# A diagonal state-space scan: B and C tables laid out as [group, channel], the scan's inputs copied to PSUM four steps at a time

## The chip, the cores and the metric

The kernel runs on one core of a Trainium2 chip. The metric is the device time of one execution in microseconds (us). Times inside an execution come from one profiled execution and count from its start. The engines are TensorE (PE, and PEld for its weight loads), VectorE (DVE), ScalarE (ACT), GpSimd (POOL) and SyncE (SP), which issues most DMAs.

## The reference

An encoder of two layers over 1040 tokens of width 1024. Layer 0 mixes tokens by a bidirectional diagonal complex state-space model (S5), layer 1 by attention, and each is followed by a SwiGLU feed-forward part. The change lies in layer 0's mixer: 64 groups of 16 channels, 64 complex states in each group, a scan forward and one backward over the tokens.

```python
def s5_direction(u, lam_re, lam_im, log_dt, b_re, b_im, c_re, c_im, reverse):
    # abr, abi: the decay exp(lambda dt); bbr, bbi: B, discretised
    bu_r = jnp.einsum('blgc,gpc->blgp', u, bbr)
    bu_i = jnp.einsum('blgc,gpc->blgp', u, bbi)
    ...
    _, _, sr, si = lax.associative_scan(_s5_combine, (a_r, a_i, bu_r, bu_i), reverse=reverse, axis=1)
    return (jnp.einsum('blgp,gcp->blgc', sr, c_re) - jnp.einsum('blgp,gcp->blgc', si, c_im))

def s5_mixer(h, ...):
    y = (s5_direction(u, ..., False) + s5_direction(u, ..., True))
    y = y.reshape(bsz, L, D_MODEL) + d_skip * hf
    g = jax.nn.gelu(y, approximate=False)
    return (g * jax.nn.sigmoid(g @ w_glu)) @ w_out
```

## The kernel before

The mixer works in blocks of T = 8 tokens, of which there are NK = 130. The 128 partitions hold 64 states of the forward direction and 64 of the backward one. It has these parts, in the order in which they are written; each engine runs its own instructions strictly in that order, and semaphores make it wait for the others.

**Parameters.** `param_T` turns B and C with TensorE into tables `bT` and `cT`, laid out as [partition, channel, real or imaginary, group]; ScalarE copies them out of PSUM (line 206). GpSimd adds real and imaginary parts into `Hs` (B) and `Cs` (C). GpSimd also makes three tables for C's side (lines 106 to 111 and 303, 304), which ScalarE completes (line 307).

**G batches.** Sixteen times, for four groups each, `g_batch` makes B times powers of the decay: three multiplies on VectorE (lines 335 to 337), which read the tables of B with group and channel exchanged, and two sums (338, 339). TensorE turns the products, ScalarE copies them to `W` (345), and `x_batch` multiplies them with the tokens `U`; ScalarE copies the result to `XS` (357), the inputs of the scan, one column pair for each block of tokens. In between, `xg_copy` and `x_main` (183, 191) turn the rest of x.

**E batches.** Sixteen times, `e_batch` makes C times powers of the decay on GpSimd: lines 386, 387 and 389 are multiplies that read the tables of C with group and channel exchanged, 388 and 390 are sums. The first four stand in GpSimd's queue near the end of the G batches. The other twelve are written into the scan's loop, one in every 7.9 steps.

**The scan.** 128 steps on VectorE, each of six instructions for two halves of the groups: a multiply of the last state with the decay `SB`, which lies in PSUM, into `TA` in SBUF (line 494); `TA` plus the step's input, back into `TA` (496); the sum with the crossed part into `XS` (498), in the place of the input.

**Work inside the scan's loop.** In rounds of four groups, one in every 6.2 steps, `inside` makes the part of the output that stays within a block. Counted from its first step, a round makes `dI` on GpSimd (424); after 2 steps TensorE multiplies B's tables with E (433); after 6 steps ScalarE copies the product to `f0` and `Z` (439 to 441), and GpSimd adds `dI` (442, 443); after 8, SyncE issues eight DMAs from `Z` to `M0` (449); after 18, TensorE multiplies `M0` with `U` (455); after 21, ScalarE copies the result back to `U` (460). There is one `f0`, so a round's copy waits until GpSimd has read that of the round before; there are two `Z`, so it waits for the DMAs of the round before the last. In the second half of the scan `swap` (467, 470, 471) reverses the backward direction's states in place, four blocks at a time, with a copy over PSUM.

**After the scan**, TensorE multiplies all states with E (521), VectorE adds to `U`, and the rest of the network follows.

PSUM has eight banks: seven in the pool `s5_ps` (`bank()`), one for `SB`.

Of the kernel before, what the change touches and what calls it, by code (L numbers as in the profile page):

```python
# [9 lines left out]
FP32 = mybir.dt.float32  # L10
# [3 lines left out]
ALU = mybir.AluOpType  # L14
PSUM = bass.MemoryType.PSUM
# [4 lines left out]
G = 64  # L20
# [5 lines left out]
CH = 16  # L26
T = 8
NK = L // T


def bc(ap, dim, n):

    a = ap.unsqueeze(dim)
    shape = list(a.shape)
    shape[dim] = n
    return a.to_broadcast(shape)
# [77 lines left out]
def s5_phase(nc, tc, P, a, ident, acc, xres, ydram, late):  # L114

    V, A, PE, PO = nc.vector, nc.scalar, nc.tensor, nc.gpsimd
    ps = P("s5_ps", bufs=7, space=PSUM)

    psc = P("s5_psc", space=PSUM)

# [8 lines left out]
    tab = P("s5_tab")  # L129
    tab2 = P("s5_tab2")  # L130
# [43 lines left out]
    for k in range(2):  # L174
        nc.sync.dma_start(out=XT[64 * k:64 * k + 64],
                          in_=a["x"][0, 1008 + T * k:1008 + T * k + T, :].rearrange("t (g c) -> g t c", c=CH))
# [20 lines left out]

    def param_T(x, raw):

        PT = tab.tile([128, CH, 2, G], FP32, name=x + "T")  # L200
        for h in range(4):
            b = bank()
            for c4 in range(4):
                c = 4 * h + c4
                transpose(b[:, c4 * 128:c4 * 128 + 128], raw[:, c::CH] if x == "b" else raw[:, c * 128:c * 128 + 128])
            A.copy(out=PT[:, 4 * h:4 * h + 4], in_=b.rearrange("p (c i g) -> p c i g", c=4, g=G))
        return PT[:, :, 0], PT[:, :, 1]

    load_x(2)
    raw_c = load_param("c")  # L210
# [37 lines left out]
        x_main(p, XG0[:, 4 * p:4 * p + 4])  # L248
    Br, Bi = param_T("b", raw_b)
    x_tail()  # L250
    Hs = tab2.tile([128, CH, G], FP32, name="Hs")
    PO.tensor_tensor(out=Hs, in0=Br, in1=Bi, op=ALU.add)
    AC = pc.tile([64, 4, 128], FP32, name="AC")
    cm, nr, sh, sn, t1, t2, rden = (t[n] for n in ("cm", "nr", "sh", "sn", "t1", "t2", "rden"))
# [17 lines left out]
    b = bank()  # L272
# [40 lines left out]
    b = bank()  # L313
    transpose(b[:CH, :G], dsr)
    A.copy(out=dsk, in_=b[:CH, :G])
    Cs = tab.tile([128, CH, G], FP32, name="Cs")

    SB = psc.tile([128, 512], FP32, name="SB")[:, :256].rearrange("p (j c g) -> p j c g", j=2, g=G)
    A.copy(out=SB[:, 0], in_=bc(PW[:, 0, 8], 1, 2))
# [9 lines left out]
    def g_batch(gb):  # L329
        gs = slice(NB * gb, NB * gb + NB)  # L330
        shp = [128, NB, T, CH]
        q_r, q_s, q_d = (bc(q[:, :, gs].rearrange("p s g -> p g s"), 3, CH) for q in G3)
        h_r, h_i, h_s = (bc(h[:, :, gs].rearrange("p c g -> p g c"), 2, T) for h in (Br, Bi, Hs))
        k1, k2, k3 = (gp.tile(shp, FP32, tag=f"k{i}", name=f"k{i}") for i in range(3))
        V.tensor_tensor(out=k1, in0=h_s, in1=q_r, op=ALU.mult)
        V.tensor_tensor(out=k2, in0=h_i, in1=q_s, op=ALU.mult)
        V.tensor_tensor(out=k3, in0=h_r, in1=q_d, op=ALU.mult)
        V.tensor_tensor(out=k2, in0=k1, in1=k2, op=ALU.subtract)
        V.tensor_tensor(out=k3, in0=k1, in1=k3, op=ALU.add)
        W = gp.tile([128, NB, 2, 128], FP32, tag="W", name="W")  # L340
        for c2, src in enumerate((k2, k3)):
            b = bank()
            for j in range(NB):
                transpose(b[:, j * 128:(j + 1) * 128], src[:, j].rearrange("p s c -> p (s c)"))
            A.copy(out=W[:, :, c2, :], in_=b.rearrange("p (g m) -> p g m", g=NB))
        return W
# [32 lines left out]
    def e_batch(gb):  # L379

        gs = slice(NB * gb, NB * gb + NB)
        g0 = NB * gb % (G // 2)
        q_r, q_s, q_d = (bc(q[:, :, gs].rearrange("p s g -> p g s"), 3, CH) for q in E3)
        c_r, c_i, c_s = (bc(c[:, :, gs].rearrange("p c g -> p g c"), 2, T) for c in (Cr, Ci, Cs))
        er, ei = (Eh[2 * gb // NG][:, i, g0:g0 + NB] for i in range(2))
        PO.tensor_tensor(out=ek, in0=c_s, in1=q_r, op=ALU.mult)
        PO.tensor_tensor(out=er, in0=c_i, in1=q_s, op=ALU.mult)
        PO.tensor_tensor(out=er, in0=ek, in1=er, op=ALU.subtract)
        PO.tensor_tensor(out=ei, in0=c_r, in1=q_d, op=ALU.mult)
        PO.tensor_tensor(out=ei, in0=ei, in1=ek, op=ALU.subtract)  # L390
# [29 lines left out]
    def inside(gb):  # L420

        gs = slice(NB * gb, NB * gb + NB)
        dI = rp.tile([CH, NB, CH], FP32, tag="dI", name="dI")
        PO.tensor_tensor(out=dI, in0=bc(ident[:CH, :CH], 1, NB), in1=bc(dsk[:, gs], 2, CH), op=ALU.mult)
        yield 2

        b = bank()
        for j in range(NB):
            g = NB * gb + j
            for c2, src in enumerate((Br, Bi)):  # L430
                for d in range(2):
                    r = slice(64 * d, 64 * d + 64)
                    PE.matmul(b[32 * d:32 * d + CH, j * 128:(j + 1) * 128], src[r, :, g],
                              E(c2, g)[r].rearrange("p s c -> p (s c)"), start=(c2 == 0), stop=(c2 == 1))
        yield 6
        Z = rp.tile([CH, NB, 2 * T - 1, CH], FP32, tag="Z", name="Z", bufs=2)
        bv = b[:64].rearrange("p (g s c) -> p g s c", g=NB, s=T)
        f0 = rp.tile([CH, NB, CH], FP32, tag="f0", name="f0")
        A.copy(out=f0, in_=bv[0:16, :, 0, :])
        A.copy(out=Z[:, :, 0:T, :], in_=bv[32:48])  # L440
        A.copy(out=Z[:, :, T:, :], in_=bv[0:16, :, 1:T, :])
        PO.tensor_tensor(out=dI, in0=dI, in1=f0, op=ALU.add)
        PO.tensor_tensor(out=Z[:, :, T - 1, :], in0=Z[:, :, T - 1, :], in1=dI, op=ALU.add)
        yield 8
        M0 = rp.tile([128, NB, 128], FP32, tag="M0", name="M0", bufs=2)
        Zf = Z.rearrange("p g s c -> p g (s c)")
        for t in range(T):
            o = (T - 1 - t) * CH
            nc.sync.dma_start(out=M0[CH * t:CH * t + CH], in_=Zf[:, :, o:o + 128])
        yield Y_AT  # L450
        banks = []
        for j0 in range(0, NB, 2):
            b = bank()
            for j in range(2):
                PE.matmul(b[:, j * NK:(j + 1) * NK], M0[:, j0 + j], U[:, NB * gb + j0 + j, :], start=True, stop=True)
            banks.append(b)
        yield Y_AT + 3
        for j0, b in zip(range(0, NB, 2), banks):
            g = NB * gb + j0
            A.copy(out=U[:, g:g + 2, :], in_=b[:, :2 * NK].rearrange("p (g k) -> p g k", g=2))  # L460
# [14 lines left out]
    sw = [(lo, hi) for hi, lo in zip(cuts, cuts[1:])]  # L475
    begun = []
    halves = [slice(0, G // 2), slice(G // 2, G)]
    for i in range(2, NK):
        for gb in range(NG):
            if i == 2 + int(E_PACE * (gb - EARLY)):  # L480
# [4 lines left out]
        for gb in list(work):  # L485
            if i >= work[gb][1]:
# [2 lines left out]
                    del work[gb]  # L489
                else:  # L490
                    work[gb][1] = 3 + int(L_PACE * gb) + at
        st, nx = XS[:, i - 1], XS[:, i]
        for h, gs in enumerate(halves):
            V.tensor_tensor(out=TA[:, h], in0=SB[:, :, :, gs], in1=bc(st[:, :, gs], 1, 2), op=ALU.mult)  # L494
        for h, gs in enumerate(halves):
            V.tensor_tensor(out=TA[:, h, 0], in0=TA[:, h, 0], in1=nx[:, :, gs], op=ALU.add)  # L496
        for h, gs in enumerate(halves):
            V.tensor_tensor(out=nx[:, :, gs], in0=TA[:, h, 0], in1=TA[:, h, 1, ::-1], op=ALU.add)  # L498
        if sw and len(begun) < 2 and i > NK // 2:
            begun.append((sw[0][0], swap(*sw.pop(0))))  # L500
            next(begun[-1][1])
# [1075 lines left out]
```

## Time and profile before

| | |
|---|---|
| median of 3 runs | 2938.03 us (2931.74 to 2938.48) |
| the profiled execution, its own time | 2936.13 us |
| its span | 2934.4 us |
| busy in the span: PE, DVE, ACT, POOL | 91%, 56%, 39%, 20% |
| granted TensorE clock, mean | 0.955 of full speed |

The parameters take to 28 us, the G batches to some 111 us, the scan to some 323 us. The remaining 2600 us (the readout, GLU, attention, feed-forward parts) are bound by TensorE.

In rows of groups of instructions, "x16" is a count. In a timeline a row has the start, the time from its first start to its last end, the engine, line and operation, output and input tiles and their shape, the count of merged instructions, and in brackets the idle time before it and what ended that. Several instructions in a row on one engine overlap by some 0.07 us, so the time from start to start is shorter than the duration.

### The profile page before, as it was taken

What the parts mean: (1) busy time and instruction counts of PE and PEld (TensorE: products, weight loads), DVE (VectorE), ACT (ScalarE), POOL (GpSimd) and SP (SyncE); (2) the same over time, 40 slices, a digit from 0 to 9 for tenths busy, and PEclk for the clock granted to TensorE, in tenths of its full rate; (3) what the DMA queues carried; (4) which work ended last, traced back from release to release, by engine and by line L of the source; (5) the groups of instructions that cost most, each with busy time, mean ns of one, the idle gap of its engine ahead of it and who ended that gap; (6) DMA issues with size and microseconds to landing.
All of it is one profiled execution on the core that took longest, in us unless ns stands there. A gap on an engine that the chain in (4) does not pass through costs nothing.

```text
span 2934.4 us, 43407 instructions
## 1 busy us (share of the span) xinstructions
PE 2656.4 (91%) x17277; PEld 2551.9 (87%) x17277; DVE 1651.7 (56%) x3270; ACT 1153.1 (39%) x2138; POOL 584.0 (20%) x544
## 2 busy tenths in 40 slices
PE   5543689999999999998998998999999999999997
PEld 4432689999999999997997887888999999999996
DVE  8999545573333333337867888887364333333334
ACT  5523353432222112125557777776332121211215
POOL 3983023230000000004204343432230000000002
PEclk8865799999999999998999999999999999999998
DMA  5110375221111111111301121111111111111101
GB/s 120 27 37 16 90 228 177 72 90 63 50 49 46 44 44 44 44 44 58 102 15 37 23 48 27 45 23 60 50 42 52 51 44 51 44 51 44 44 30 58
DMA packets 124837, 167.42 MB, mean 57 GB/s; under 512 B 13499, under 2 KB 104971, under 8 KB 124635
## 3 DMA queue, kind: packets, MB, share of 16 engines
q1 hardware_dynamic: 118203, 141.22, 17.0%
q0 software_dynamic: 5712, 21.30, 2.1%
q8 instruction: 136, 2.23, 0.3%
q10 hardware_dynamic: 720, 2.13, 0.2%
q14 instruction: 66, 0.54, 0.1%
HBM read 126.41 MB, written 21.23 MB: 50 GB/s over the span
## 4 chain that ended last, share of the span: by engine, by line
PE 74%; DVE 16%; ACT 3%; issue 3%; DMA 2%; POOL 1%; SPq 0%; ACTq 0%; DVEq 0%; POOLq 0%
PE bk L682 21%; PE bk L683 21%; PE bk L684 21%; PE pv L1094 4%; PE pt L1072 3%; DVE XS L498 3%; DVE TA L496 3%; DVE mx L1052 3%; DVE pl L1085 2%; PE b L521 2%; DVE TA L494 2%; ACT ph L1080 1%; ACT P L1056 1%; DVE acc L738 1%; PE bk L904 1%
## 5 line engine op out<-in xcount | busy, mean ns | idle before, releaser
L682 PE MATMUL bk<-Hh,unit 128*128 128x348 f32 (+1 forms) x2928 | 956.3, 327 | 9.8 <-ACT Hh L772 6.2
L683 PE MATMUL bk<-Hl,unit 128*128 128x348 f32 (+1 forms) x2928 | 945.4, 323 | 1.1 <-DVE Hl L776 1.0
L684 PE MATMUL bk<-Hh,unit 128*128 128x348 f32 (+1 forms) x2928 | 943.8, 322 | 0.0
L682 PEld LDWEIGHTS bk<-Hh,unit 128*128 128x128 f32 x2928 | 555.2, 190 | 15.1 <-ACT Hh L772 5.8
L683 PEld LDWEIGHTS bk<-Hl,unit 128*128 128x128 f32 x2928 | 554.9, 190 | 6.3 <-DVE Hl L776 2.0
L684 PEld LDWEIGHTS bk<-Hh,unit 128*128 128x128 f32 x2928 | 554.8, 189 | 0.0
L846 DVE TENSOR_TENSOR sg<-sg,bk 128x348 f32<-128x348 f32 x132 | 68.1, 516 | 631.3 <-PE bk L684 623.5
L711 POOL TENSOR_TENSOR lns<-lns,lnsq 128x348 f32<-128x348 f32 (+1 forms) x72 | 70.0, 981 | 1552.2 <-ACT lnsq L709 1551.1
L682 PE MATMUL bk<-gt,unit 128*128 128x348 f32 (+1 forms) x1056 | 340.3, 322 | 0.0
L684 PE MATMUL bk<-gt,unit 128*128 128x348 f32 (+1 forms) x1056 | 338.9, 321 | 0.0
L683 PE MATMUL bk<-gt,unit 128*128 128x348 f32 (+1 forms) x1056 | 338.2, 320 | 0.0
L869 DVE TENSOR_TENSOR acc<-acc,bk 128x348 f32<-128x348 f32 (+1 forms) x480 | 237.5, 513 | 112.7 <-PE bk L684 112.7
L848 ACT CAST gt<-sg 128x348 fp32r<-128x348 f32 x132 | 63.6, 482 | 489.1 <-DVE sg L846 489.1
L1072 PE MATMUL pt<-ident,P 128*116 128x128 f32 (+1 forms) x1188 | 181.7, 279 | 44.8 <-DVE pl L1085 40.5
L1085 DVE TENSOR_TENSOR pl<-pt,ph 116x512 fp32r<-116x512 f32 (+3 forms) x340 | 204.4, 619 | 15.1 <-ACT ph L1080 13.4
L1060 POOL TENSOR_SCALAR P<-P,l 128x1044 f32<-128x1044 f32 x132 | 149.8, 1147 | 292.5 <-PE pv L1094 167.7
L1072 PEld LDWEIGHTS pt<-ident,P 128*116 128x116 f32 (+1 forms) x1188 | 133.0, 136 | 81.1 <-issue 30.7
L683 PEld LDWEIGHTS bk<-gt,unit 128*128 128x128 f32 x1056 | 198.7, 188 | 0.5 <-issue 0.2
L682 PEld LDWEIGHTS bk<-gt,unit 128*128 128x128 f32 x1056 | 198.7, 188 | 0.5 <-issue 0.2
L684 PEld LDWEIGHTS bk<-gt,unit 128*128 128x128 f32 x1056 | 198.5, 188 | 0.0
L1080 ACT CAST ph<-pt 116x512 fp32r<-116x512 f32 (+3 forms) x340 | 168.9, 535 | 74.4 <-PE pt L1072 60.1
L597 ACT CAST unit<-raw 128x1024 fp32r<-128x1024 f32 x110 | 113.1, 1046 | 212.9 <-DMA raw<-in_ffn_w_up_dram 168.4
(285 smaller groups left out, 4123.1 us busy)
## 6 DMA issues: line engine op xcount, KB each, us to landing
raw<-in_ffn_w_gate_dram SPq DMA_DIRECT2D x44, 512.0 KB
raw<-in_ffn_w_up_dram SPq DMA_DIRECT2D x44, 512.0 KB
raw<-in_ffn_w_down_dram SPq DMA_DIRECT2D x44, 512.0 KB
y<-xdram SPq DMA_DIRECT2D x16, 520.0 KB
QA<-QH SPq DMA_DIRECT2D x30, 260.0 KB
raw<-in_attn_w_qkv_dram SPq DMA_DIRECT2D x14, 512.0 KB
xdram<-acc SPq DMA_DIRECT2D x32, 130.0 KB
xres<-xn POOLq DMA_DIRECT2D x8, 520.0 KB, 5.1
```

Source lines behind the costliest of these rows:

```text
L496: V.tensor_tensor(out=TA[:, h, 0], in0=TA[:, h, 0], in1=nx[:, :, gs], op=ALU.add)
L498: V.tensor_tensor(out=nx[:, :, gs], in0=TA[:, h, 0], in1=TA[:, h, 1, ::-1], op=ALU.add)
L597: A.copy(out=u[:, 0], in_=r)
L682: mm(out, wh, xh, start=(first and i == 0), stop=False)
L683: mm(out, wh, xl, start=False, stop=False)
L684: mm(out, wl, xh, start=False, stop=(last and i == n - 1))
L869: V.tensor_tensor(out=x, in0=x, in1=b, op=ALU.add)
L1060: PO.tensor_scalar(out=k.P, in0=k.P, scalar1=k.l, scalar2=1.0, op0=ALU.mult, op1=ALU.mult)
L1072: PE.transpose(b[:m, w * i + 128 * x:w * i + 128 * x + 128], u.P[x][:, KB_N * kt:KB_N * kt + m], self.ident)
L1080: A.copy(out=u.ph[s][:m, :w], in_=u.t[s][:m, :w])
L1085: V.tensor_tensor(out=u.pl[s][:m, :w], in0=u.t[s][:m, :w], in1=u.ph[s][:m, :w].bitcast(FP32), op=ALU.subtract)
L1094: PE.matmul(u.o[:, :u.w], VAs[u.j][:m, kt], (u.ph, u.pl)[x][s][:m, c:c + u.w], start=(kt == 0 and x == 0), stop=(kt == KBS - 1 and x == 1))
```

## The change

The tables of B and C, `Hs` and `Cs` are laid out as [group, channel], with channels next to each other; ScalarE's copy in `param_T` writes them in that order. The slices in `g_batch`, `e_batch` and the matmul of `inside` follow.

A new function `inputs` lets ScalarE copy the scan's inputs of four steps from `XS` into a PSUM tile of one bank, of which there are two. It is called for steps 2 to 5 ahead of the loop, and at every fourth step i (2, 6, 10 and so on) for steps i + 4 to i + 7, behind the other work of step i. The scan's first add puts `TA` plus the input back into that PSUM tile, and the second adds that and the crossed half of `TA` into `XS`. For the two banks, the pool `s5_ps` shrinks from seven to five.

```diff
-    ps = P("s5_ps", bufs=7, space=PSUM)
+    ps = P("s5_ps", bufs=5, space=PSUM)
...
-        PT = tab.tile([128, CH, 2, G], FP32, name=x + "T")
+        PT = tab.tile([128, 2, G, CH], FP32, name=x + "T")
...
-            A.copy(out=PT[:, 4 * h:4 * h + 4], in_=b.rearrange("p (c i g) -> p c i g", c=4, g=G))
-        return PT[:, :, 0], PT[:, :, 1]
+            A.copy(out=PT[:, :, :, 4 * h:4 * h + 4], in_=b.rearrange("p (c i g) -> p i g c", c=4, g=G))
+        return PT[:, 0], PT[:, 1]
...
-        h_r, h_i, h_s = (bc(h[:, :, gs].rearrange("p c g -> p g c"), 2, T) for h in (Br, Bi, Hs))
+        h_r, h_i, h_s = (bc(h[:, gs], 2, T) for h in (Br, Bi, Hs))
...
-        c_r, c_i, c_s = (bc(c[:, :, gs].rearrange("p c g -> p g c"), 2, T) for c in (Cr, Ci, Cs))
+        c_r, c_i, c_s = (bc(c[:, gs], 2, T) for c in (Cr, Ci, Cs))
...
+    IN = {}
+
+    def inputs(i):
+
+        n = min(4, NK - i)
+        t = psc.tile([128, 4, 2, G], FP32, tag="in", name="IN", bufs=2)
+        A.copy(out=t[:, :n], in_=XS[:, i:i + n])
+        for k in range(n):
+            IN[i + k] = t[:, k]
+
+    inputs(2)
     for i in range(2, NK):
...
-        st, nx = XS[:, i - 1], XS[:, i]
+        if i % 4 == 2 and i + 4 < NK:
+            inputs(i + 4)
+        st, nx, bi = XS[:, i - 1], XS[:, i], IN.pop(i)
         for h, gs in enumerate(halves):
             V.tensor_tensor(out=TA[:, h], in0=SB[:, :, :, gs], in1=bc(st[:, :, gs], 1, 2), op=ALU.mult)
         for h, gs in enumerate(halves):
-            V.tensor_tensor(out=TA[:, h, 0], in0=TA[:, h, 0], in1=nx[:, :, gs], op=ALU.add)
+            V.tensor_tensor(out=bi[:, :, gs], in0=TA[:, h, 0], in1=bi[:, :, gs], op=ALU.add)
         for h, gs in enumerate(halves):
-            V.tensor_tensor(out=nx[:, :, gs], in0=TA[:, h, 0], in1=TA[:, h, 1, ::-1], op=ALU.add)
+            V.tensor_tensor(out=nx[:, :, gs], in0=bi[:, :, gs], in1=TA[:, h, 1, ::-1], op=ALU.add)
```

The order of GpSimd's and TensorE's instructions stays as it was. ScalarE's queue early in the scan's loop, before the change, from the first round's Z on (line 439 copies a round's f0, 440 and 441 its Z):

```order
L440 COPY Z_1333<-b_1287 16x4x128
L441 COPY Z_1333<-b_1287 16x4x112
L439 COPY f0_1405<-b_1363 16x64
L440 COPY Z_1404<-b_1363 16x4x128
L441 COPY Z_1404<-b_1363 16x4x112
L439 COPY f0_1487<-b_1439 16x64
L440 COPY Z_1486<-b_1439 16x4x128
L441 COPY Z_1486<-b_1439 16x4x112
```

and with it, from the same place (line 484 copies inputs into PSUM, here for steps 14, 18, 22 and 26 and the three behind each):

```order
L440 COPY Z_1339<-b_1291 16x4x128
L441 COPY Z_1339<-b_1291 16x4x112
L484 COPY IN_1354<-XS_391 128x512
L484 COPY IN_1406<-XS_391 128x512
L439 COPY f0_1415<-b_1371 16x64
L440 COPY Z_1414<-b_1371 16x4x128
L441 COPY Z_1414<-b_1371 16x4x112
L484 COPY IN_1472<-XS_391 128x512
L439 COPY f0_1499<-b_1449 16x64
L440 COPY Z_1498<-b_1449 16x4x128
L441 COPY Z_1498<-b_1449 16x4x112
L484 COPY IN_1513<-XS_391 128x512
```

The input copies of the scan now stand between the rounds' copies: that for steps 22 to 25 behind the second round's f0 and Z, that for steps 26 to 29 behind the third round's.

VectorE's queue, the last sum of the G batches and the scan's first step, before:

```order
L338 TENSOR_TENSOR k1_1151<-k0_1150,k1_1151 128x512
L339 TENSOR_TENSOR k2_1152<-k0_1150,k2_1152 128x512
L494 TENSOR_TENSOR TA_1261<-SB_384,XS_391 128x128 x2
L496 TENSOR_TENSOR TA_1261<-TA_1261,XS_391 128x64 x2
L498 TENSOR_TENSOR XS_391<-TA_1261 128x2x32 x2
```

and after:

```order
L338 TENSOR_TENSOR k1_1151<-k0_1150,k1_1151 128x512
L339 TENSOR_TENSOR k2_1152<-k0_1150,k2_1152 128x512
L507 TENSOR_TENSOR TA_1261<-SB_384,XS_391 128x128 x2
L509 TENSOR_TENSOR IN_1262<-TA_1261,IN_1262 128x2x32 x2
L511 TENSOR_TENSOR XS_391<-IN_1262,TA_1261 128x2x32 x2
```

Nothing moved here; SB and IN lie in PSUM, TA and XS in SBUF, so each instruction of a step now has one input from either memory.

## Rows read from the trace of the kernel before

**Rows 1.** The chain that ended last, 0 to 345 us, its shares by line
```profile
by line: DVE XS L498 23.4%; DVE TA L496 21.7%; DVE TA L494 14.8%; issue 7.8%; PE b L521 6.2%; DVE k L337 4.4%; DVE k L336 3.5%; DVE k L335 3.4%; DMA XT<-in_x_dram 2.9%; DVE k L338 2.3%; DVE k L339 2.2%; PE b L126 0.7%; SPq L167 0.7%; SPq L1
```
**Rows 2.** Table by stretches: length, busy PE, PEld, DVE, ACT, POOL (instructions), clock, DMA
```profile
115.00:210.00 95.00, 43.33 (x430) 32.57 (x426) 94.02 (x163) 18.65 (x47) 89.58 (x93) 0.73 0.13 28
...
280.00:323.00 43.00, 14.12 (x100) 11.15 (x100) 42.87 (x269) 25.89 (x56) 3.13 (x9) 0.58 0.17 44
```
**Rows 3.** The same for line 494 alone: length, busy DVE (instructions, two a step)
```profile
115.00:210.00 95.00, 13.11 (x55) 0.73 0.13 28
...
250.00:280.00 30.00, 6.65 (x28) 0.56 0.13 27
```
**Rows 4.** The scan's three lines, the whole scan: duration min/median/max in ns
```profile
L494 DVE TENSOR_TENSOR TA<-SB,XS x256: 271/276/292, 115.4 to 322.0; 128x128 f32<-128x128 f32 x128
...
L496 DVE TENSOR_TENSOR TA<-TA,XS x256: 205/211/2996, 116.5 to 322.3; 128x64 f32<-128x64 f32 x128
...
L498 DVE TENSOR_TENSOR XS<-TA x256: 208/211/2966, 117.7 to 322.6; 128x64 f32<-128x64 f32 x128
```
**Rows 5.** Timeline, VectorE and GpSimd in one step from 128 us
```profile
128.38 1.38 POOL L389 TENSOR_TENSOR E<-cT,E 128x512 f32<-128x512 f32 x1
...
128.82 1.15 DVE L496 TENSOR_TENSOR TA<-TA,XS 128x64 f32<-128x64 f32 x2
129.84 1.26 POOL L390 TENSOR_TENSOR E<-E,ek 128x512 f32<-128x512 f32 x1
```
**Rows 6.** Timeline, VectorE in one step from 312 us, with GpSimd idle
```profile
312.42 0.47 DVE L494 TENSOR_TENSOR TA<-SB,XS 128x128 f32<-128x128 f32 x2
312.82 0.34 DVE L496 TENSOR_TENSOR TA<-TA,XS 128x64 f32<-128x64 f32 x2
313.08 0.34 DVE L498 TENSOR_TENSOR XS<-TA 128x64 f32<-128x64 f32 x2
313.36 0.47 DVE L494 TENSOR_TENSOR TA<-SB,XS 128x128 f32<-128x128 f32 x2
```
**Rows 7.** Lines of the G batches, duration min/median/max in ns
```profile
L335 DVE TENSOR_TENSOR k<-Hs,G x16: 1047/1058/2064, 28.2 to 106.2; 128x512 f32<-128x512 f32 x16
...
L337 DVE TENSOR_TENSOR k<-bT,G x16: 1056/1330/3079, 30.1 to 108.3; 128x512 f32<-128x512 f32 x16
...
L338 DVE TENSOR_TENSOR k<-k,k x16: 668/670/1712, 31.1 to 109.5; 128x512 f32<-128x512 f32 x16
```
**Rows 8.** Timeline, ScalarE in the G batches: starts of two and two rounds
```profile
79.76 0.63 ACT L191 COPY acc<-b 128x512 f32<-128x512 f32 x1
...
83.63 0.66 ACT L191 COPY acc<-b 128x512 f32<-128x512 f32 x1
...
92.91 1.13 ACT L345 COPY W<-b 128x512 f32<-128x512 f32 x2 [1.05 <-PE b L126]
...
97.44 1.13 ACT L345 COPY W<-b 128x512 f32<-128x512 f32 x2 [1.04 <-PE b L126]
```
**Rows 9.** Timeline, GpSimd: the first operations of three E batches
```profile
76.48 35.58 POOL L386 TENSOR_TENSOR ek<-Cs,E 128x512 f32<-128x512 f32 x1 [21.37 <-ACT E L307]
...
117.61 1.37 POOL L386 TENSOR_TENSOR ek<-Cs,E 128x512 f32<-128x512 f32 x1
...
124.39 1.36 POOL L386 TENSOR_TENSOR ek<-Cs,E 128x512 f32<-128x512 f32 x1
```
**Rows 10.** Timeline, ScalarE: the second round's f0, the third round's Z
```profile
151.79 0.20 ACT L439 COPY f<-b 16x64 f32<-16x64 f32 x1 [31.05 <-POOL dI L442]
...
159.00 0.58 ACT L440 COPY Z<-b 16x512 f32<-16x512 f32 x1 [5.75 <-DMA M<-Z]
```
**Rows 11.** Timeline, copies of the swaps: into PSUM, within SBUF, out of PSUM
```profile
281.11 0.59 ACT L467 COPY b<-XS 64x512 f32<-64x512 f32 x1
...
322.94 0.29 DVE L470 COPY XS<-XS 64x256 f32<-64x256 f32 x1
...
323.67 0.43 DVE L471 COPY XS<-b 64x256 f32<-64x256 f32 x1 [0.44 <-ACT XS L471]
```

More of the change, by code (lines that the diff above doesn't have):

```diff
@@ L250, in s5_phase @@
     x_tail()
-    Hs = tab2.tile([128, CH, G], FP32, name="Hs")
+    Hs = tab2.tile([128, G, CH], FP32, name="Hs")
     PO.tensor_tensor(out=Hs, in0=Br, in1=Bi, op=ALU.add)
@@ L315, in s5_phase @@
     A.copy(out=dsk, in_=b[:CH, :G])
-    Cs = tab.tile([128, CH, G], FP32, name="Cs")
+    Cs = tab.tile([128, G, CH], FP32, name="Cs")
     SB = psc.tile([128, 512], FP32, name="SB")[:, :256].rearrange("p (j c g) -> p j c g", j=2, g=G)
@@ L432, in inside @@
                     r = slice(64 * d, 64 * d + 64)
-                    PE.matmul(b[32 * d:32 * d + CH, j * 128:(j + 1) * 128], src[r, :, g],
+                    PE.matmul(b[32 * d:32 * d + CH, j * 128:(j + 1) * 128], src[r, g],
                               E(c2, g)[r].rearrange("p s c -> p (s c)"), start=(c2 == 0), stop=(c2 == 1))
```

## The prediction

> **What bounds the kernel now.** I read the chain that ended last, then a table by stretches, then single instructions. Until the readout that follows the mixer's scan the chain is almost wholly VectorE's, and the scan's three lines lead it [rows 1]. The table says why: from 115 to 210 us VectorE is never idle, yet passes only 55 / 2 = 27.5 steps, while GpSimd is busy for 89.58 of 95 us [rows 2, 3]; from 250 to 280 it passes 14. Where GpSimd has nothing to do, one step takes 313.36 - 312.42 = 0.94 us [rows 6].
>
> What VectorE does in the long steps is seen from the durations [rows 4]. The add lines 496 and 498 have a median of 211 ns and a maximum near 3 us. The multiply of line 494, with twice the elements, never takes over 292 ns in the same stretch. The difference is in the operands: line 494 reads one tensor from PSUM and one from SBUF and writes SBUF; the adds read two from SBUF. While GpSimd streams, a pair of adds is through only when the operation that GpSimd has begun is over [rows 5]. So the adds wait for GpSimd, and line 494 does not. The waits cost 95 - 27.5 x 0.94 = 69 us and 30 - 14 x 0.94 = 17 us, together 86 us of a scan whose 128 steps would take 120. GpSimd isn't slowed by this: its operations keep 1.26 to 1.38 us [rows 5, 9].
>
> **The change, part by part.** *The scan's adds.* Both adds now have one PSUM operand, so by the form of line 494 they stop waiting. Line 498's successor has exactly that form (PSUM and SBUF in, SBUF out). What an operand in PSUM costs by itself: the two multiplies of a step take 0.40 us, the two adds 0.26 [rows 6]; 2 x 64 more elements at 1.04 ns explain 0.13 of the 0.14, so reading PSUM adds nothing there. Writing PSUM from VectorE is in no row. The bound above is a copy of one shape that reads PSUM instead of SBUF, 0.43 against 0.29 us, 140 ns more [rows 11]; below, ScalarE's copies of 512 elements take 0.59 into PSUM [rows 11] and 0.58 into SBUF [rows 10], no gain to speak of. I take zero, since line 494 is the nearest row, and keep 0 to 140 ns for each of four adds.
>
> The Trainium skill speaks against this: its Perfetto Trace Analysis, section Optimizing Scalar/DVE Operations, gives a VectorE operation some 60 ns of access overhead on SBUF and some 125 on PSUM. By the difference, an estimate of 65 ns on four adds, a step would take 1.20 us and and the time would be near the middle price of the first rival below; by that rule the trace doesn't agree, since line 494's rows show no such excess.
>
> *The copies.* ScalarE gets 32 copies of 512 elements, some 0.59 us each like line 467 [rows 11], 19 us in all. It is busy 25.89 of 43 us where it has most to do [rows 2], and 11 copies more make that 32: hidden as work. But they are a new **wait**. VectorE can't begin step i + 4 before the copy that stands in ScalarE's queue behind the other work of step i, and that work waits for GpSimd. Before, ScalarE sat 31.05 us for GpSimd before the second f0 copy, and 5.75 us for the DMAs that read Z before the third Z copy [rows 10], and VectorE didn't care. Now the copy for steps 22 to 25 stands behind that f0, and the one for 26 to 29 behind that Z.
>
> This sets the scan's start, counted from the moment when GpSimd gets the port. Before, that was at 76.48 + 35.58 - 1.37 = 110.7 us [rows 9], and f0 came at 151.79, 41.1 us later, after six E batches of 6.78 us. *The tables* take the long strides from three of five operations of a batch, whose excess over the other two is 0.1 us [rows 5, 9]: 1.8 us less, 39.3. Then three copies (1.4) and the input copy (0.6): step 22 begins at 41.3. The Z copy came 159.00 - 151.79 = 7.2 us after f0; with two Z copies (1.2) and the input copy, step 26 begins at 39.3 + 7.2 + 1.8 = 48.3. The other 104 steps take 98 us: 146. GpSimd keeps just ahead: 16 batches of 6.5 us and three small operations in each of 16 rounds, 11 us, make 115 us, and its last result is asked for at step 102, at 119.7. For so small a margin I add 3 us: **149 us after GpSimd gets the port**.
>
> *The G batches.* Lines 335 to 337 read with long strides and take 1.06 to 1.33 us where line 338 takes 0.67 [rows 7]. With runs of 16 they should take 0.67 too, and a batch 3.0 us instead of 4.5. ScalarE is next: its round takes 83.63 - 79.76 = 3.87 us while x is being turned, and 97.44 - 92.91 - 1.04 = 3.49 after that [rows 8]. From the fifth batch on, 7 x 3.87 + 5 x 3.49 = 44.5 replaces 12 x 4.5 = 54; of the first four, which GpSimd's tables slow, some 2.5 us go. So the scan's first input comes about 12 us earlier, at 104. VectorE, now ahead of ScalarE by up to two batches, ends its part some 2 us earlier still: GpSimd gets the port at 110.7 - 14 = 96.5, and the scan ends at 96.5 + 149 = 245.5. Before, it ended at 322.8, just ahead of the copy of 322.94 that closes it [rows 11].
>
> There is a second order of events: GpSimd gets the port earlier, in a gap of VectorE, and then both take turns. A contiguous operation of a G batch takes 1.71 us in such a turn, the maximum of line 338 [rows 7]. Some 20 such operations would be left, 34 us instead of 14: the scan begins at some 121, but four E batches are done by then, the early waits fall away, and it ends at 121 + 120 + 3 = 244. Both orders give the same end, so I needn't choose.
>
> *What is lost.* The copies of B and C to the new tables write runs of four elements; I allow 2 us for them, though ScalarE has idle time near both. The bank pool shrinks from seven to five: in the G part TensorE is the one that runs ahead, and in the scan two swaps, one round's product and two of Y make five. Cost nothing; if that cover fails, a round waits for a swap, about four steps, inside the range. The readout and all behind it only move.
>
> **Sum.** 322.8 - 245.5 - 2 = 75 us. From the profiled execution's 2936.1 that gives 2861; the median of the runs lies 1.9 higher: **2863 us**.
>
> **The rivals.** *PSUM adds cost more.* At half of the bound, 70 ns, a step takes 0.94 + 4 x 0.07 = 1.22 us; the scan ends at 96.5 + 48 + 127 = 272, 51 us gained, 2887. At the whole bound, 1.50: 300, 23 us, 2915. For it: no row writes PSUM from VectorE, and one add reads and writes the same bank. Against: line 494. *The waits move to ScalarE's queue.* If each of the some 13 rounds after step 26 stalls VectorE as the first ones do, by 1 to 5 us, say 3, that is 39 us: 2902. For it: the margin of 4 us above. Against: behind the first rounds GpSimd needs less time for each than VectorE does. *The G part gains nothing*, being held by ScalarE or TensorE: 110.7 + 149 = 260, 61 gained, 2877. *Slower: the change doesn't remove the wait*, since it comes from the SBUF access as such and not from the second read. Then the scan keeps its 207 us, and pays for PSUM from zero to 4 x 128 x 140 ns = 72; in the middle, less 12 from the G part, 2938 + 36 - 12 = 2962. It turns to a loss from 12 / 512 = 23 ns per add. Against it stands line 494, which touches SBUF twice and never waits.
>
> **How the numbers follow.** The forecast has 0.59, the dearer PSUM adds 0.16 (0.08 of it near the middle price, 0.02 at a sum near no change), ScalarE's queue 0.15, the G part without gain 0.07, the loss 0.03. The forecast's own errors: 10 us below, if GpSimd slips into gaps without harm, and 15 above. So the range is 2850 to 2892; it leaves out the dear half of the PSUM case, part of the queue's and the loss, and something below. A measurement of this kernel tells 0.3%, 9 us, from no change: faster 0.95, same 0.02, slower 0.03.
>
> **What would show it.** In the changed profile both add lines should have a maximum close to their median, some 210 ns, while GpSimd works: if the PSUM-writing one stands at 280 or more, the first rival holds. VectorE should be idle in the scan, for ScalarE's input copies, first before steps 22 and 26, by some 20 us in all; much idle time after that is the second rival. Lines 335 to 337 should take 0.67 to 0.7 us, and the scan should end near 245 us. Adds that still take 1 us or more beside GpSimd would make the prediction wrong altogether.

## The result and the profile after

| | before | after |
|---|---|---|
| median of 4 runs each, us | 2936.31 (2931.74 to 2938.48) | 2884.59 (2882.68 to 2889.59) |
| ratio | | 0.9829 (95%: 0.9810 to 0.9847) |
| the profiled execution, us | 2936.13 | 2882.80 |
| its span, us | 2934.4 | 2881.0 |
| start of the readout's matmuls, us | 323.7 | 270.8 |

The change gains 51.7 us, and the two profiled executions differ by 53.3. The scan ends 52.9 us earlier (269.96 against 322.81), so nearly all of it lies ahead of the readout: from the readout's first matmul to the end the two kernels need 2610.7 and 2610.2 us. I had forecast 2863, a gain of 75: the time is 22 us above that, within the range.

First the whole scan of the changed kernel, by its three lines (count, duration min/median/max in ns, first and last start); they answer to [rows 4].

```profile
L507 DVE TENSOR_TENSOR TA<-SB,XS x255: 278/280/292, 117.8 to 268.9; 128x128 f32<-128x128 f32 x128
...
L509 DVE TENSOR_TENSOR IN<-TA,IN x256: 218/228/230, 118.5 to 269.3; 128x64 f32<-128x64 f32 x128
...
L511 DVE TENSOR_TENSOR XS<-IN,TA x256: 211/220/225, 119.0 to 269.7; 128x64 f32<-128x64 f32 x128
```

The maxima near 3 us are gone from both adds: not one of 512 waits for GpSimd any more. Yet the table by stretches, for line 507 alone (length, busy DVE and its instructions, two a step), has 155 / 2 = 77.5 steps in 92 us and 50 in 60:

```profile
118.00:210.00 92.00, 36.89 (x155) 0.72 0.16 33
210.00:270.00 60.00, 23.85 (x100) 0.62 0.16 40
```

That is 1.19 and 1.20 us a step. The same two stretches for all engines (length, busy PE, PEld, DVE, ACT, POOL with their instructions, clock, DMA):

```profile
118.00:210.00 92.00, 49.68 (x478) 40.08 (x474) 86.26 (x464) 38.86 (x88) 62.77 (x83) 0.72 0.16 33
210.00:270.00 60.00, 20.14 (x154) 16.06 (x148) 56.45 (x304) 37.32 (x76) 13.43 (x20) 0.62 0.16 40
```

GpSimd is busy for 62.77 of the 92 us in the first and for 13.43 of the 60 in the second, and the step is the same. Before, it was 3.45 with GpSimd busy and 0.94 without. So the long step isn't GpSimd's doing. The timeline of one late step shows where it is; it answers to [rows 6] (start, time from the first start to the last end, engine, line, tiles, count of merged instructions).

```profile
264.14 0.28 DVE L507 TENSOR_TENSOR TA<-SB,XS 128x128 f32<-128x128 f32 x1
264.34 0.22 DVE L509 TENSOR_TENSOR IN<-TA,IN 128x64 f32<-128x64 f32 x1
...
264.59 0.23 DVE L509 TENSOR_TENSOR IN<-TA,IN 128x64 f32<-128x64 f32 x1
264.86 0.35 DVE L511 TENSOR_TENSOR XS<-IN,TA 128x64 f32<-128x64 f32 x2
265.13 0.28 DVE L507 TENSOR_TENSOR TA<-SB,XS 128x128 f32<-128x128 f32 x1
```

Read the starts. The two adds of line 511 start a pair that gives way to the next line after 0.27 us, as every pair of adds did before. But line 509's second add starts 0.25 us after its first, which by then (0.22 us) is over, and line 511's first starts 0.27 us after that, when the second (0.23) is over. Two handovers that used to overlap by half no longer do: 0.12 us each, 0.245 a step, 31 us in 128 steps. Each half of the state has its own columns of the tile IN, but the tile is one PSUM bank for both: the second half's add writes the bank that the first half's is writing, and line 511's first add reads the bank that the second half's is writing. That was a reading; the experiments test it.

Last the waits of VectorE and of ScalarE in the scan (line that waited, for what, us in total, times, longest):

```profile
DVE TA L507 <- ACT XS L357: 0.4, 1, 0.4
DVE IN L509 <- ACT IN L484: 0.3, 1, 0.3
DVE IN L509 <- DVE IN L509: 0.2, 1, 0.2
...
ACT IN L484 <- DVE XS L511: 50.7, 17, 4.2
```

VectorE hardly waits: the stalls that I had forecast before steps 22 and 26 aren't there, and ScalarE's input copies wait for VectorE's steps instead. Why is seen in the G batches. First lines 335 and 337 (duration min/median/max in ns), which answer to [rows 7]:

```profile
L335 DVE TENSOR_TENSOR k<-Hs,G x16: 672/680/1757, 29.5 to 103.0; 128x512 f32<-128x512 f32 x16
...
L337 DVE TENSOR_TENSOR k<-bT,G x16: 672/684/2834, 30.7 to 106.0; 128x512 f32<-128x512 f32 x16
```

GpSimd's timeline in the same stretch, with the idle time before a row and what ended it in brackets, answers to [rows 9]:

```profile
70.71 3.48 POOL L386 TENSOR_TENSOR ek<-Cs,E 128x512 f32<-128x512 f32 x1 [14.90 <-ACT E L307]
80.77 1.11 POOL L387 TENSOR_TENSOR E<-cT,E 128x512 f32<-128x512 f32 x1 [6.58 <-PE b L126]
81.96 1.60 POOL L388 TENSOR_TENSOR E<-ek,E 128x512 f32<-128x512 f32 x1
...
110.50 1.43 POOL L386 TENSOR_TENSOR ek<-Cs,E 128x512 f32<-128x512 f32 x1
```

And VectorE's, where the G batches end and the scan begins:

```profile
109.22 1.75 DVE L339 TENSOR_TENSOR k<-k,k 128x512 f32<-128x512 f32 x1
117.19 0.29 DVE L507 TENSOR_TENSOR TA<-SB,XS 128x128 f32<-128x128 f32 x1 [6.22 <-PE b L355]
117.85 0.29 DVE L507 TENSOR_TENSOR TA<-SB,XS 128x128 f32<-128x128 f32 x1 [0.37 <-ACT XS L357]
```

Contiguous, lines 335 to 337 take 0.68 us as forecast. But VectorE, now faster, runs out of work now and then (from 70 to 90 us it is busy for 18.71 of 20 us; before, for all 20), and in such a gap GpSimd gets in: its first E batch operation takes 3.48 us where it was held for 35.58 before. From some 81 us on both engines take turns, at 1.4 to 1.76 us an operation. The last G batch ends at 110.97, as before (110.8), but four of GpSimd's sixteen E batches are done by then. This is the second order of events of the prediction.

### The profile page after: what moved, and what is told of

Read it like the earlier page. It is cut to its first block, busy times and chain, and to the rows that moved or that the text cites. A ratio compares the mean times of both kernels' runs of the same rounds, so it can differ in the third digit from the quotient of the medians.

```text
span 2881.0 us, 43478 instructions
## 1 busy us (share of the span) xinstructions
PE 2660.3 (92%) x17277; PEld 2560.6 (89%) x17277; DVE 1586.5 (55%) x3270; ACT 1168.4 (41%) x2170; POOL 545.2 (19%) x544
## 4 chain that ended last, share of the span: by engine, by line
PE 77%; DVE 14%; ACT 4%; issue 3%; DMA 1%; POOL 1%; SPq 0%; ACTq 0%; POOLq 0%; DVEq 0%
PE bk L696 21%; PE bk L695 21%; PE bk L697 21%; PE pv L1107 4%; PE pt L1085 3%; DVE mx L1065 2%; DVE pl L1098 2%; PE b L534 2%; DVE IN L509 2%; DVE TA L507 2%; DVE XS L511 2%; ACT ph L1093 1%; DVE acc L751 1%; ACT P L1069 1%; PE bk L917 1%
```

## The experiments

Times are medians of 4 runs, ratios against the kernel before on the same chip. The kernel before takes 2936.2 to 2936.6 us on each of them, so times of different experiments can be compared.

**tables_only** undoes the scan's part, with the copies of the inputs (their lines are left out here) and the pool of five banks; the tables stay.

```
-            V.tensor_tensor(out=bi[:, :, gs], in0=TA[:, h, 0], in1=bi[:, :, gs], op=ALU.add)
+            V.tensor_tensor(out=TA[:, h, 0], in0=TA[:, h, 0], in1=nx[:, :, gs], op=ALU.add)
...
-            V.tensor_tensor(out=nx[:, :, gs], in0=bi[:, :, gs], in1=TA[:, h, 1, ::-1], op=ALU.add)
+            V.tensor_tensor(out=nx[:, :, gs], in0=TA[:, h, 0], in1=TA[:, h, 1, ::-1], op=ALU.add)
```

> The new tables alone, with the scan as it was before the change. Theory: the G part gains nothing net, because GpSimd slips into VectorE's gaps and both take turns; the scan's first input comes near 117 us as in the changed kernel, but four E batches are done by then. With both adds waiting for GpSimd as before, some 12 E batches are left to collide with; the scan then ends near 303 to 308 us, a gain of 15 to 20 us: 2917 to 2921 us. Rival: the tables matter for nothing in time, the scan ends at 322 as before: 2936. Second rival: the G part gains the forecast's 12 us besides, since ScalarE's copies of inputs are not there to disturb anything: the scan begins near 104 and the time is about 2924 (before less 12), with lines 335 to 337 at 0.68 us in all cases.

Measured: 2908.52 us, ratio 0.9906 (0.9891 to 0.9921), a gain of 28 us. The scan's first step stands at 119.6 us, as in the order of turns, and its last ends at 295.3. The order of events is the theory's, but the gain is larger than its 15 to 20 us: the time lies 8.5 us below its range. The table by stretches for line 494 gives 43 / 2 = 21.5 steps in 60 us beside GpSimd, and 46 steps in 43 us (0.93 each) while GpSimd does nothing:

```profile
120.00:180.00 60.00, 10.04 (x43) 0.86 0.21 43
180.00:223.00 43.00, 22.24 (x92) 0.51 0.02 4
```

GpSimd's idle time there is a wait for ScalarE's copy to f0, which stands behind the first swap's copy (line 467), and that waits 44.9 us for VectorE's steps:

```profile
224.40 0.41 POOL L442 TENSOR_TENSOR dI<-dI,f 16x64 f32<-16x64 f32 x1 [44.72 <-ACT f L439]
```

A step beside GpSimd takes 2.8 us instead of 3.45. Line 386 of GpSimd has a median of 1.09 us where it had 1.35: the tables shorten three of its five operations, by more than the 0.1 us that I had allowed, and VectorE's waits for them would be shorter too. That this is the whole of the larger gain is not shown.

**scan_only** is the other half: the new scan on the old tables. Against the changed kernel (the slices follow the tables and are left out here):

```
-        PT = tab.tile([128, 2, G, CH], FP32, name=x + "T")
+        PT = tab.tile([128, CH, 2, G], FP32, name=x + "T")
...
-    Cs = tab.tile([128, G, CH], FP32, name="Cs")
+    Cs = tab.tile([128, CH, G], FP32, name="Cs")
```

> The old tables with the new scan. Theory: the G batches keep their 4.5 us and GpSimd gets the port only after them, at about 110.8 us; a scan step takes 1.185 us as in the changed kernel, with no add above 0.3 us; and since the first f0 now comes some 40 us after the scan's first steps, VectorE is idle before steps 22 and 26 by 10 to 15 us together. The scan ends near 115 + 152 + 13 = 280 us, 43 us before the old end: about 2893 to 2898 us. Rival, the waits in ScalarE's queue never bind: the scan ends near 267 and the time is that of the changed kernel, 2884. Rival, they bind in every round at 3 us each: beyond 2920.

Measured: 2896.21 us, 0.9862 (0.9848 to 0.9877), a gain of 40 us; the scan ends at 284.2. GpSimd is held until 111.5 again (its first E batch operation starts at 77.38 and takes 35.51 us, 1.38 of them its own). VectorE's timeline has the forecast stalls, in brackets the idle time and what ended it:

```profile
154.49 0.49 DVE L509 TENSOR_TENSOR IN<-TA,IN 128x64 f32<-128x64 f32 x2 [13.01 <-ACT IN L484]
161.47 0.49 DVE L509 TENSOR_TENSOR IN<-TA,IN 128x64 f32<-128x64 f32 x2 [2.16 <-ACT IN L484]
```

ScalarE's timeline just ahead of these two shows what its copies stood behind:

```profile
152.63 0.20 ACT L439 COPY f<-b 16x64 f32<-16x64 f32 x1 [20.34 <-POOL dI L442]
...
159.84 0.58 ACT L440 COPY Z<-b 16x512 f32<-16x512 f32 x1 [5.24 <-DMA M<-Z]
```

From the first input 20 steps of 1.185 us lead to step 22, and 4 more to step 26. f0 comes 152.63 - 111.5 = 41.1 us after GpSimd is let through, Z 7.2 after that: the times of [rows 10], which the prediction carried over. With the copies behind them in ScalarE's queue, VectorE now pays 15.2 us for it. That is the difference to the changed kernel, whose scan begins some 0.8 us later and ends 14.3 us earlier: with the new scan the tables are worth only the absence of these two stalls, 11.6 us of the whole time. So the parts' gains, 28 and 40, don't add up to 52; both get rid of the same collisions.

**after_hold** makes the order of events that the prediction had worked out first. VectorE writes a few elements of GpSimd's scratch tile behind its last G operation, and the first four E batches are issued only then.

```
-            for b in range(EARLY):
-                e_batch(b)
...
+        if gb + 2 == NG:
+            V.memset(ek[:, 0, 0], 0.0)
+            for b in range(EARLY):
+                e_batch(b)
```

> The changed kernel with the first four E batches held back until VectorE's last G operation but one. This makes the other of the two orders of events: GpSimd doesn't slip in. Theory, as in the prediction: the scan begins at about 104 us instead of 117.9, GpSimd gets the port near 97, and VectorE is idle before steps 22 and 26 for ScalarE's copies. At 1.185 us a step the end is the larger of 104 + 152 = 256 and of what those waits add, some 10 us: 256 to 268, that is 2871 to 2883 us. Rival, both orders give the same end: 2883. Second rival, the G part is bound by ScalarE's rounds or TensorE, and the scan begins no earlier than 115: the waits then come on top and the time is 2890 or more.

Measured: 2873.49 us, 0.9784 (0.9770 to 0.9799), 11 us faster than the changed kernel. VectorE's timeline:

```profile
96.40 0.07 DVE L407 MEMSET ek<- 128x16 f32 x1
103.78 0.29 DVE L509 TENSOR_TENSOR TA<-SB,XS 128x128 f32<-128x128 f32 x1 [7.31 <-PE b L355]
104.76 0.29 DVE L509 TENSOR_TENSOR TA<-SB,XS 128x128 f32<-128x128 f32 x1 [0.69 <-ACT XS L357]
...
134.81 0.49 DVE L511 TENSOR_TENSOR IN<-TA,IN 128x64 f32<-128x64 f32 x2 [5.67 <-ACT IN L486]
...
141.80 0.49 DVE L511 TENSOR_TENSOR IN<-TA,IN 128x64 f32<-128x64 f32 x2 [2.16 <-ACT IN L486]
```

VectorE's part of the G batches ends at 96.4 (forecast 96.5) and GpSimd begins, the scan begins at 104.8 (104), and the stalls stand before the steps named. The scan ends at 264.6, so the two orders are 5 us apart at this step, not equal. The profiled executions are 7 us apart; the rest of the 11 us is not explained, and the runs of each kernel differ by 5 to 7 us among themselves.

**products_psum** asks what makes the step long. The products, not the inputs, lie in PSUM, one bank for each half; no copies of inputs are needed (their lines are left out here), and every operation still has at most one SBUF input.

```
-    TA = rp.tile([128, 2, 2, 2, G // 2], FP32, name="TA")
+    TA = [psc.tile([128, 512], FP32, name=f"TA{h}")[:, :128].rearrange("p (j c g) -> p j c g", j=2, c=2) for h in range(2)]
+    TS = rp.tile([128, 2, 2, G // 2], FP32, name="TS")
...
+            V.tensor_tensor(out=TA[h], in0=SB[:, :, :, gs], in1=bc(st[:, :, gs], 1, 2), op=ALU.mult)
+            V.tensor_tensor(out=TS[:, h], in0=TA[h][:, 0], in1=nx[:, :, gs], op=ALU.add)
+            V.tensor_tensor(out=nx[:, :, gs], in0=TS[:, h], in1=TA[h][:, 1, ::-1], op=ALU.add)
```

> The new tables, but the scan has no copies of its inputs: the multiply writes its products to PSUM, one bank for each half, the first add reads PSUM and the input in SBUF and writes SBUF, the second reads SBUF and PSUM and writes SBUF. No operation has two SBUF inputs, and no two operations of different halves touch one bank. Theory, the step of 1.185 us is long because the second half's first add waits until the first half's, which writes the same bank, is done (0.25 us a step): here nothing of the kind is left, a step takes 0.94 to 0.98 us, the scan ends near 117.9 + 124 = 242 us and the time is about 2856. Rival, a write to PSUM is dear by itself (0.12 us for each of the two that write it): the multiplies here write PSUM, a step takes about 1.18 us again, and the time is about 2884. Second rival: the multiply, reading and writing PSUM, is slowed by GpSimd or by its size beyond that, 2890 and more.

Measured: 2851.85 us, 0.9709 (0.9693 to 0.9725). A step in the timeline, with GpSimd working beside it:

```profile
200.49 0.49 DVE L495 TENSOR_TENSOR TA<-SB,XS 128x128 f32<-128x128 f32 x2
200.89 0.35 DVE L497 TENSOR_TENSOR TS<-TA,XS 128x64 f32<-128x64 f32 x2
201.15 0.34 DVE L499 TENSOR_TENSOR XS<-TS,TA 128x64 f32<-128x64 f32 x2
201.41 0.49 DVE L495 TENSOR_TENSOR TA<-SB,XS 128x128 f32<-128x128 f32 x2
```

0.925 us a step, all along; the scan ends at 240.3. Here all six operations of a step read or write PSUM and the multiplies write it, and the step is no longer than the 0.94 of [rows 6]. A multiply that writes PSUM has a median of 292 ns against 276 before, but the next starts no later for it. So writing PSUM isn't dear, and the rival falls.

**products_one_bank** is the same kernel with both halves' products in one bank.

```
-    TA = [psc.tile([128, 512], FP32, name=f"TA{h}")[:, :128].rearrange("p (j c g) -> p j c g", j=2, c=2) for h in range(2)]
+    TB = psc.tile([128, 512], FP32, name="TB")
+    TA = [TB[:, 128 * h:128 * h + 128].rearrange("p (j c g) -> p j c g", j=2, c=2) for h in range(2)]
```

> The products in PSUM as in the run with one bank for each half, but now both halves' products in one bank and nothing else changed. Theory, sharing is what costs: the second half's multiply waits for the first's, which writes the same bank (0.1 us or a little more), and the first half's add, which reads the bank, for the second's multiply (0.12): a step goes from 0.925 to 1.15 to 1.3 us, the scan gets 30 to 48 us longer, and the time is 2882 to 2900 us. Rival, the position in the banks doesn't matter and the changed kernel's long step came from its add reading and writing one place: the step stays at 0.925 and the time at 2852.

Measured: 2904.99 us, 0.9891 (0.9876 to 0.9906): 53 us for nothing but the place. The step:

```profile
200.76 0.63 DVE L496 TENSOR_TENSOR TB<-SB,XS 128x128 f32<-128x128 f32 x2
201.43 0.36 DVE L498 TENSOR_TENSOR TS<-TB,XS 128x64 f32<-128x64 f32 x2
201.70 0.34 DVE L500 TENSOR_TENSOR XS<-TS,TB 128x64 f32<-128x64 f32 x2
202.08 0.63 DVE L496 TENSOR_TENSOR TB<-SB,XS 128x128 f32<-128x128 f32 x2
```

1.32 us, 0.40 more, and a time 5 us over the expected range. There are three handovers that don't overlap: the two that I had named, which make the multiplies' pair 0.67 from start to start instead of 0.40, and a third that I hadn't: the next step's multiply writes the bank that the last add has just read (0.38 instead of 0.26).

**two_banks** does it to the changed kernel itself: the inputs of the two halves in two banks, eight steps to a copy, made only at the step that needs it, so that VectorE waits for it. The first add still writes where it reads.

```
-        t = psc.tile([128, 4, 2, G], FP32, tag="in", name="IN", bufs=2)
-        A.copy(out=t[:, :n], in_=XS[:, i:i + n])
+        ts = [psc.tile([128, 8, 2, G // 2], FP32, tag=f"in{h}", name=f"IN{h}") for h in range(2)]
+        for t, gs in zip(ts, halves):
+            A.copy(out=t[:, :n], in_=XS[:, i:i + n, :, gs])
```

> The changed kernel with the inputs of the two halves in two PSUM banks instead of one, eight steps to a copy (which is waited for, since nothing else is in reserve, some 1.3 us per eight steps, 21 us in all). The first add still reads and writes its bank in place. Theory, the long step comes from the two halves sharing a bank, so that the second half's add waits for the first half's, and the first half's second add, which reads the bank, for the second half's: both waits go, a pair of first adds takes 0.26 to 0.27 us from start to start of the next pair instead of 0.52, a step 0.94, and the time is 2884 - 31 + 21 = about 2874 us, less or more with the copies. Rival, in-place use of a PSUM bank, or the write by itself, costs 0.12 us for each: the pair stays at 0.52, a step at 1.185, and with the copies' waits the time is about 2905.

Measured: 2866.73 us, 0.9765 (0.9748 to 0.9781), faster than the changed kernel in spite of 11.4 us in which VectorE waits for the copies (I had expected some 21 us of waits and 2874). The step:

```profile
176.02 0.48 DVE L508 TENSOR_TENSOR TA<-SB,XS 128x128 f32<-128x128 f32 x2
176.41 0.35 DVE L510 TENSOR_TENSOR IN<-TA,IN 128x64 f32<-128x64 f32 x2
176.67 0.35 DVE L512 TENSOR_TENSOR XS<-IN,TA 128x64 f32<-128x64 f32 x2
176.94 0.48 DVE L508 TENSOR_TENSOR TA<-SB,XS 128x128 f32<-128x128 f32 x2
```

Its waits for the copies in the scan (line that waited, for what, us in total, times, longest):

```profile
DVE IN L510 <- ACT IN L485: 11.4, 29, 1.7
```

0.92 us: the add that reads and writes one place in PSUM costs nothing, once the halves don't share the bank. These three runs settle, in both directions, that the long step comes from two halves that share a bank which one of them writes.

The traces also tell what holds an operation back there. They record for each instruction whether it waits for a semaphore, though not for which count. Here, and in the kernel before, each of the six operations of every step has such a wait. In the changed kernel the second add of line 511 has none in all 128 steps, and in products_one_bank the second add of line 498 has none. An instruction needs no wait of its own where the one ahead of it has already waited for as much. So line 511's first add waits, in the program itself, for line 509's second, though it reads other columns. It starts 34 to 36 ns after that one's end, and the other handovers named start 34 or 35 ns after an end in nearly every step, where those that overlap start 70 to 95 ns before it. So one handover of each step is shown to be a wait in the program's semaphores, which the kernel's text doesn't name; of the others the equal time only suggests it. No run leaves these waits out, so whether VectorE would have to wait without them stays open. It also stays open whether the waits go by the bank or by the tile: every PSUM tile of this kernel takes a whole bank, so the two can't be parted here. In SBUF both halves shared one tile before the change, and the step was 0.94.

**sum_sbuf** gives the second add two SBUF inputs again.

```
-            V.tensor_tensor(out=bi[:, :, gs], in0=TA[:, h, 0], in1=bi[:, :, gs], op=ALU.add)
+            V.tensor_tensor(out=TA[:, h, 0], in0=TA[:, h, 0], in1=bi[:, :, gs], op=ALU.add)
...
-            V.tensor_tensor(out=nx[:, :, gs], in0=bi[:, :, gs], in1=TA[:, h, 1, ::-1], op=ALU.add)
+            V.tensor_tensor(out=nx[:, :, gs], in0=TA[:, h, 0], in1=TA[:, h, 1, ::-1], op=ALU.add)
```

> The changed kernel, but the first add writes its sum to SBUF and not back to PSUM; the second add then has two SBUF inputs again. Theory: the two waits in the shared bank go, so that a step takes 0.94 us where GpSimd is idle; the first add never waits for GpSimd (maximum below 0.3 us), and the second, which has two SBUF inputs as before the change, does, with a maximum of 1 to 3 us. About 12 E batches and their small operations, some 80 us of GpSimd's work, lie in the scan; in it a step takes one or two of GpSimd's operations, 1.3 to 2.6 us, so that the waits cost 30 to 50 us against the 31 saved: 2880 to 2905 us. Rival, a SBUF input is what makes an operation wait, and not that there are two: then the first add, with one, waits too, and so would the multiply, and the scan goes back towards its 207 us: 2920 or more.

Measured: 2898.92 us, 0.9872 (0.9857 to 0.9886). The two adds over the whole scan (min/median/max in ns):

```profile
L509 DVE TENSOR_TENSOR TA<-TA,IN x256: 203/214/222, 120.8 to 283.1; 128x64 f32<-128x64 f32 x128
...
L511 DVE TENSOR_TENSOR XS<-TA x256: 210/222/2430, 121.1 to 283.3; 128x64 f32<-128x64 f32 x128
```

Two adds of one shape, side by side: with one SBUF input the longest of 256 takes 222 ns, with two it takes 2430. It is the second SBUF input that waits for GpSimd. The two halves' inputs lie in one bank here too, but no operation of a step writes it. The timeline of a step shows that the first adds then overlap, and the pair gives way to the next line after 0.26 us:

```profile
270.86 0.35 DVE L509 TENSOR_TENSOR TA<-TA,IN 128x64 f32<-128x64 f32 x2
271.12 0.36 DVE L511 TENSOR_TENSOR XS<-TA 128x64 f32<-128x64 f32 x2
```

**products_psum_hold** joins products_psum and the held E batches of after_hold (both edits are above).

> The products in PSUM, one bank for each half, together with the first four E batches held back to VectorE's last G operation but one. Both were measured apart: the former has a step of 0.925 us and a scan that begins at 122, since GpSimd takes turns with the G batches; the latter has the last G operation at 96.4 us and the scan's first step near 105. VectorE here waits for no ScalarE copy in the scan. Theory, the two gains add: the scan ends near 105 + 118.5 + 0.5 = 224 us, 16 us before the end of 240.4 that the former has; the time is 2835 to 2838 us. Rival: with VectorE so early, the readout's start is set by another engine (GpSimd, which starts 16 batches at 97 us and needs some 110 us, ends near 210 to 220 with its last round, then TensorE and ScalarE): the time then stays at 2843 to 2852.

Measured: 2842.64 us, 0.9680 (0.9665 to 0.9694), the fastest of all, between the 2835 to 2838 of the theory and the 2843 of the rival. VectorE's timeline at the end of the scan:

```profile
214.93 0.35 DVE L499 TENSOR_TENSOR TS<-TA,XS 128x64 f32<-128x64 f32 x2
215.20 0.34 DVE L501 TENSOR_TENSOR XS<-TS,TA 128x64 f32<-128x64 f32 x2
227.95 0.29 DVE L473 COPY XS<-XS 64x256 f32<-64x256 f32 x1 [12.41 <-ACT b L470]
```

VectorE is through at 215.5, earlier than expected, since the scan begins at 97.3. (The profiled execution, 2838.8 us, is the shortest of four that reach to 2845.2.) Then it waits 12.4 us for ScalarE, which is behind with the swaps. So the gains didn't add in full: the rival was right that another engine then sets the readout's start.

## Why the prediction was nearly right

*The adds stop waiting for GpSimd:* right, by the argument from the form of line 494. The changed kernel's maxima show it, and sum_sbuf tells the form apart from all else. The Trainium skill says the same in SBUF — State Buffer, section Who interferes with whom: outside its two-port modes, a VectorE instruction with at most one SBUF input doesn't contend with GpSimd, and one with two contends with a GpSimd instruction that reads SBUF. The traces agree: 230 ns is the longest of the adds with one (the changed kernel), 2430 that of those with two (sum_sbuf).

*A step takes 0.94 us beside GpSimd:* this is the step that failed, and it is more than the whole error of 22 us. A step takes 1.185 us, 31 us too much in 128 steps; other terms, below, gave some 9 us back. Without that luck the time would have been about 2863 + 31 = 2894, just outside the range. I had looked for a price of writing PSUM, between 0 and 140 ns for each add, and had seen that one add reads and writes the same bank, as a reason for that price. No such price shows in the step of products_psum or of two_banks. What I hadn't asked is who else touches the bank: two halves, whose operations overlapped because they were independent, were made to wait for each other once they lay in one bank.

*Rival 1, PSUM adds cost more,* gives 2887 at its middle price, 2.4 us from the result. Its number came true by chance and its reason didn't: line 509 has a median of 228 ns, against the 280 that the prediction set as its mark, and a scan whose multiplies, twice as large, write PSUM runs at 0.925. What I had cited from Perfetto Trace Analysis (Trainium skill, section Optimizing Scalar/DVE Operations), more access overhead for VectorE on PSUM than on SBUF, isn't borne out by that step either: an operation that writes PSUM takes 16 or 17 ns longer in itself (292 against 276, 228 against 211), and the step no longer.

*The copies hidden as work, and a new wait behind f0 and Z:* the mechanism is right to the step, as scan_only and after_hold show, but it doesn't bind in the changed kernel, where E batches 0 to 3 are done before the scan. The second rival, a stall in every round, doesn't show in any run.

*The G batches:* operations of 0.68 us and GpSimd's start at 96.5 are right for the order worked out first, and after_hold shows it. In the changed kernel the second order came, begun 3 us earlier than forecast (117.9 against 121). "Both orders give the same end" is off by 5 us at the real step.

*What is lost:* the copies to the new tables and the smaller bank pool cost nothing that can be seen (the G batches begin at 29.5 us against 28.2 before, but at 29.6 in scan_only, which has the old tables); the 2 us weren't needed. GpSimd's operations on the tables came out at 1.09 us, where 0.1 us less than before would be some 1.25.

The sum in terms of the second order: 244 and 2 for what is lost, less 3 for the earlier start, less 3 for the margin and 2 for the loss that didn't come, plus 31 for the handovers, is 269; measured 270.0.

## What to carry to other kernels

When an operand is moved to PSUM so that an engine need not wait for another, count who else uses that bank: two independent chains that are interleaved to hide each other's latency need a bank each, or the interleaving is lost. Among the operands that could be moved, take the one that needs no copy: moving the products cost ScalarE nothing and gave 33 us more than moving the inputs as the change does. Most of that is the shared bank; against two_banks, where the inputs have a bank for each half, it is 15 us, 11.4 of them VectorE's waits for copies. And where two parts of a change remove the same collision, don't add their gains.

## What the runs showed of the hardware

- In a row of overlapping operations VectorE writes PSUM at the pace of SBUF here: a step with all its results in SBUF takes 0.94 us, with the products in PSUM 0.925.
- Two operations of VectorE on different columns of one PSUM bank don't overlap in these programs when one of them writes it, and such a handover costs some 0.12 us. In one handover of each step the program's own semaphores are shown to order them; that the engine would have to is not shown. Two that only read a bank overlap: so do the multiplies of both halves, which read the tile SB (0.20 us apart at a duration of 0.28), the adds of line 511 of the changed kernel (0.27 us for a pair at 0.22 each) and the first adds of sum_sbuf (0.26).
- Reading the tables with long strides costs GpSimd too: 1.35 us against 1.09 for 512 elements, and VectorE 1.06 to 1.33 against 0.68.
- How GpSimd and VectorE share turned here on gaps in VectorE's row: before the change one GpSimd operation took 35.58 us beside VectorE's unbroken row, while in the changed kernel, whose row had gaps, both alternate from 81 us on at about 1.4 to 1.76 us an operation.
